# Layer 0 opened feature tile by feature tile: modulation columns of 128 features, and six gate tiles that follow each one

## The chip, the cores and the metric

The kernel runs on one core of a Trainium2 chip. The metric is device time in microseconds, the median of repeated runs. Engines are called as in the profile: PE (TensorE, matmuls; PEld its weight loads), DVE (VectorE), ACT (ScalarE), POOL (GpSimd), and SP, which issues most DMAs. [...]

## The reference

A two-layer backbone over 1024 latent tokens and 256 context tokens of 1024 features: layer 0 is windowed attention, layer 1 a bidirectional state-space mixer. What matters here is how layer 0 begins:

```python
mod = jax.nn.silu(cond) @ w + b          # cond: c (latent) or c_ctx (context); 3 x 1024 columns
shift, scale, gate = jnp.split(mod, 3, axis=-1)
u  = rms_normalize(h)  * (1.0 + scale[:, None]) + shift[:, None]
uc = rms_normalize(hc) * (1.0 + scale_c) + shift_c
q, k, v, g = jnp.split(h @ w_in, ...)    # of u and of uc; g is used as silu(g)
```

`rms_normalize` divides each token by the root of its mean square over the 1024 features.

## The kernel before

Activations lie with features on the 128 partitions, as eight feature tiles k = 0..7, and tokens along the free axis, in three token tiles: 0 and 1 (latent, 512 tokens each) and 2 (the context, 256 tokens). Every operand of a large product is split into a hi part and the rest (`uH`, `uL` for activations, `wh`, `wl` for weights), and a product is three matmuls: hi x hi, hi x lo and lo x hi (`mm3`, L227 to L229). A weight is loaded into a `wr` buffer (seven), cast to hi by ACT (L213) and reduced to its low part by POOL or DVE (L215); `wh` and `wl` have four buffers each, reused in turn. An engine's order is settled ahead of the run by a scheduler that works on a modelled timeline; `issue_after` and `high_priority` bend it.

`norm0` is the opening. It loads tile 0 of x and the modulation weights in blocks of 512 output columns (`load_ada`: four blocks of 2 MiB, shift in blocks 0 and 1, scale in 2 and 3). `ada0` multiplies a block by the two condition vectors: eight matmuls of 512 columns into four strips of 32 PSUM rows, a copy to SBUF (`arow`, L374) and four small sums (`modulation`, L201) that turn it into columns. `stats` squares a token tile on ACT and adds the eight squares, on DVE for tile 0 and on POOL for tiles 1 and 2; `rstd_c` makes sums over partitions on PE (L348), root (ACT, L356), reciprocal and a diagonal (DVE, L359), and a product with ones (PE, L361) that spreads the factor `rr` over all partitions. The eight feature tiles are then modulated in two halves of four, each half once its two blocks of columns are there. Behind each half come half the products of G0 = 4 gate tiles (`g_out` takes tanh and writes them to DRAM). The rest of the gate tiles for tile 0, and all for tile 2, are made at the end of `qkvg`.

Tiles 1 and 2 are normalised while PE makes keys and values of tile 0. `modulate` does one feature tile of one token tile (with `pool=True` POOL takes the multiplication by `rr`). `qkvg` then runs over the token tiles, keys (two products) and then values (one per 128 tokens), and after that the queries and the remaining gates, with the modulation of later stages (`adaln_col`) in between. The tiles `v`, `kHH`, `kL` lie in a pool that opens where the opening's pool `n0` closes, so their first writes wait for the last readers there. PSUM has four banks for products (`pj`).

Of the kernel before, what the change touches and what calls it, by code (L numbers as in the profile page):

```python
# [47 lines left out]
VLAST = 0  # L48
G0 = 4
N0P = (0, 4, 8)  # L50
U0OFF = (0, -200, -100)
AHEAD = 1
# [53 lines left out]
class Kernel:  # L106
# [18 lines left out]
    def build(self):  # L125
# [11 lines left out]
        self.eps = t(cp, [P, 1], F32, "eps")  # L137
        nc.vector.memset(self.eps, EPS)

        self.ptag = "pt"  # L140
        self.mod = [t(cp, [P, 24, 2], F32, f"mod{i}") for i in range(2)]
# [15 lines left out]
    def load_cond(self, p):  # L157
        nc, t, cp = self.nc, self.t, self.cp
        cc = t(p, [P, KT, 2], F32, "cc")
        nc.sync.dma_start(cc, self.a["cc"].rearrange("p (k c) -> p k c", k=KT))  # L160
        th = t(p, [P, KT, 2], F32, "cth")
        nc.scalar.activation(th, cc, AF.Tanh, scale=0.5)
        nc.vector.tensor_scalar_mul(cc, cc, 0.5)
        cs = self.csf = t(cp, [P, KT, 2], F32, "cs")
        nc.vector.scalar_tensor_tensor(cs, in0=th, scalar=1.0, in1=cc, op0=ALU.add, op1=ALU.mult)

        self.sel = t(cp, [P, 2], F32, "sel")
        nc.vector.tensor_reduce(self.sel, self.ident.rearrange("p (j r) -> p r j", r=32)[:, 0:2], axis=mybir.AxisListType.X, op=ALU.add)
        self.bada = t(cp, [P, 2, 24], F32, "bada")
        nc.sync.dma_start(self.bada, self.a["bada"].rearrange("p (l t) -> p l t", l=2))  # L170

    def adaln_col(self, layer, n, pool, ps):
# [23 lines left out]
    def modulation(self, layer, n, row, ps):  # L196

        nc = self.nc
        mt = self.t(ps, [P, 512], F32, "pt")
        for j in range(4):  # L200
            nc.tensor.matmul(mt[:, 2 * j : 2 * j + 2], row[:, j * P : (j + 1) * P], self.sel, start=True, stop=True)  # L201
        m = self.mod[layer][:, n * 4 : n * 4 + 4, :]
        nc.vector.tensor_tensor(m, mt[:, :8].rearrange("p (a b) -> p a b", b=2), self.bada[:, layer, n * 4 : n * 4 + 4].unsqueeze(2).broadcast_to([P, 4, 2]), op=ALU.add)
        if n // 2 == 1:
            nc.vector.tensor_scalar_add(m, m, 1.0)
        return m
# [74 lines left out]
    def modulate(self, layer, h, r, i, k, pool=False):  # L281
# [11 lines left out]
        else:  # L293
            nc.vector.scalar_tensor_tensor(h, in0=h, scalar=sc, in1=r, op0=ALU.mult, op1=ALU.mult)
            nc.scalar.activation(uh, h, AF.Identity, bias=sh)
            nc.vector.scalar_tensor_tensor(ul, in0=h, scalar=sh, in1=uh, op0=ALU.add, op1=ALU.subtract)

# [67 lines left out]

    def ada0(self, n, raw, ps):

        nc, t = self.nc, self.t
        pj = t(ps, [P, 512], F32, "aps", 2)
        for k in range(KT):  # L370
            j = k % 4
            nc.tensor.matmul(pj[32 * j : 32 * j + 32], self.cs[:, k, :], raw[k // 2][:, k % 2], start=k < 4, stop=k >= 4)
        row = t(self.p0, [P, 512], F32, "arow")
        nc.scalar.copy(row, pj)  # L374
        self.modulation(0, n, row, ps)

    def norm0(self, c0, p):


        nc, t, a = self.nc, self.t, self.a  # L380
        ps = self.psA
        p1 = self.p0 = self.pool("n0", ctx=c0, side="right")

        u = self.up
        hin, hs = {}, {}
        raws = {}

        def load_x(i):
            src = self.xin(i).rearrange("(k p) n -> p k n", p=P)
            if i == 0:  # L390
                x = t(u, [P, KT, 512], F32, "uL1")
                hin[i] = [x[:, :4], x[:, 4:]]
            elif i == 1:
                hin[i] = [t(u, [P, KT // 2, 512], F32, tag) for tag in ("uH2", "uL2")]
            else:
                hin[i] = [t(p1, [P, 2, 512], F32, "wada").rearrange("p k n -> p (k n)").rearrange("p (k n) -> p k n", k=4) for _ in range(2)]
            hs[i] = [x[:, k] for x in hin[i] for k in range(4)]
            for e in range(2):
                ld = nc.sync.dma_start(hin[i][e], src[:, 4 * e : 4 * e + 4])
            return ld  # L400

        def load_ada(n):
            raws[n] = [t(p1, [P, 2, 512], F32, "wada") for e in range(4)]
            for e in range(4):
                ld = nc.sync.dma_start(raws[n][e], self.a["w_ada"][0, n, 2 * e : 2 * e + 2].rearrange("k p c -> p k c"))
            return ld

        def stats(i):
            n = TT[i][1]
            acc = t(p1, [P, 512], F32, "sqa")[:, :n]  # L410
            for k in range(KT):
                if k == 0:
                    nc.scalar.activation(acc, hs[i][k], AF.Square)
                else:
                    sq = t(p1, [P, 512], F32, "sqt")[:, :n]
                    nc.scalar.activation(sq, hs[i][k], AF.Square)
                    (nc.vector if i in (0,) else nc.gpsimd).tensor_tensor(acc, acc, sq, op=ALU.add)
            return self.rstd_c(p1, acc, n, D)

        def gates(e):  # L420
            return [self.load_w(a["wg"][x][:, e * 512 : (e + 1) * 512], 4, eng=nc.gpsimd) for x in range(G0)]

        last = lambda: self.tc.issue_after(ld.ins)
        load_x(0)
        load_ada(0)
        ld = load_ada(2)
        with last():
            wg = gates(0)
        r = stats(0)
        for k in range(KT):  # L430
            nc.vector.tensor_mul(hs[0][k], hs[0][k], r)
        self.alloc_u(0)
        m = self.mod[0]
        for e in range(2):
            for n in (e, 2 + e):
                self.ada0(n, raws[n], ps)
            for k in range(4 * e, 4 * e + 4):
                h, uh = hs[0][k], self.uH[0][:, k, :]
                nc.vector.tensor_scalar(out=h, in0=h, scalar1=m[:, 8 + k, 0:1], scalar2=m[:, k, 0:1], op0=ALU.mult, op1=ALU.add)
                nc.scalar.copy(uh, h)  # L440
                nc.vector.tensor_sub(self.uL[0][:, k, :], h, uh)  # L441
            if e == 0:
                pj = [t(ps, [P, 512], F32, "pj") for _ in range(G0)]
            for x in range(G0):
                self.mm3(pj[x], [(wg[x][0][:, k], wg[x][1][:, k], self.uH[0][:, 4 * e + k, :], self.uL[0][:, 4 * e + k, :]) for k in range(4)], e == 0, e == 1)
                if e == 1:
                    self.g_out(p, pj[x], x, 0)
            if e == 0:
                load_ada(1)
                ld = load_ada(3)  # L450
                with last():
                    wg = gates(1)
                    wk = [self.load_halves(a["wk"][x], nc.gpsimd) for x in range(2)]
                    ld = load_x(1)
                with last():
                    self.load_rope(p, 0, LAT)
                    load_x(2)
        for i in (1, 2):
            with self.tc.high_priority(offset=-U0OFF[i]):
                r = stats(i)  # L460
                self.alloc_u(i)
                for k in range(KT):
                    self.modulate(0, hs[i][k], r, i, k, N0P[i] > k)
        return wk
# [11 lines left out]
    def load_rope(self, p, s, n):  # L476
# [3 lines left out]
        self.nc.sync.dma_start(self.cos, self.a["cos"][:, s : s + n])  # L480
        self.nc.sync.dma_start(self.sin, self.a["sin"][:, s : s + n])

# [23 lines left out]
    def g_out(self, p, pj, x, i):  # L506
        nc, t = self.nc, self.t
        n = TT[i][1]
        th = t(p, [P, 512], F32, "qf")[:, :n]
        nc.scalar.activation(th, pj[:, :n], AF.Tanh, scale=0.5)  # L510
        nc.vector.scalar_tensor_tensor(th, in0=th, scalar=1.0, in1=pj[:, :n], op0=ALU.add, op1=ALU.mult)
        nc.sync.dma_start(self.sg_d[x // 2][i][x % 2], th)

    def q_step(self, p, w, x, i):
# [972 lines left out]
def layout(i):  # L1487
# [10 lines left out]
    d["cc"] = np.ascontiguousarray(cc.reshape(KT, P, 2).transpose(1, 0, 2)).reshape(P, -1)  # L1498
    d["w_ada"] = np.ascontiguousarray(i["w_ada"].reshape(2, KT, P, 6, 512).transpose(0, 3, 1, 2, 4))
    d["bada"] = np.ascontiguousarray(i["b_ada"].reshape(2, 24, P).transpose(2, 0, 1)).reshape(P, 48)  # L1500
    w = i["attn_w_in"][0]
# [3 lines left out]
    perm = np.concatenate([np.arange(h * HD, (h + 1) * HD) for j in range(KV) for e in range(2) for h in (4 * j + e, 4 * j + 2 + e)])  # L1505
    d["wg"] = tiles(w[:, 1536:][:, perm])
    d["wo"] = tiles(i["attn_w_out"][0][perm])
    d["sink"] = np.ascontiguousarray(i["attn_sink"].reshape(1, HEADS))
# [43 lines left out]
```

## Time and profile before

| | us |
|---|---|
| median of 3 runs | 1890.34 |
| lowest, highest run | 1886.82, 1890.70 |
| span of the profiled execution | 1886.0 |
| PE busy in it | 1790.8 |

The profiled execution's own time is its span, first to last instruction; nothing else of it is listed. It lies 0.8 us below the fastest run and 4.3 below the median. A profile row names line, engine, operation, the tile written and the tiles read; "idle before" is how long the engine had stood still, with the instruction or DMA that released it. Starts are in microseconds from the span's start.

### The profile page before, as it was taken

What the parts mean: (1) busy time and instruction counts of PE and PEld (TensorE: products, weight loads), DVE (VectorE), ACT (ScalarE), POOL (GpSimd) and SP (SyncE); (2) the same over time, 40 slices, a digit from 0 to 9 for tenths busy, and PEclk for the clock granted to TensorE, in tenths of its full rate; (3) what the DMA queues carried; (4) which work ended last, traced back from release to release, by engine and by line L of the source; (5) the groups of instructions that cost most, each with busy time, mean ns of one, the idle gap of its engine ahead of it and who ended that gap; (6) DMA issues with size and microseconds to landing.
All of it is one profiled execution on the core that took longest, in us unless ns stands there. A gap on an engine that the chain in (4) does not pass through costs nothing. (4 is left out here: it accounts for less than half of the span.)

```text
span 1886.0 us, 29647 instructions
## 1 busy us (share of the span) xinstructions
PE 1790.8 (95%) x10632; PEld 1543.2 (82%) x10632; DVE 1186.5 (63%) x2214; ACT 906.5 (48%) x1863; POOL 751.1 (40%) x1026
## 2 busy tenths in 40 slices
PE   6779998899999899879999999999999999999997
PEld 3678776788889787668898898989889898988887
DVE  4753425887777766584665757666575766754743
ACT  4522225677787765472353534434353543543532
POOL 2731105664456464302334352524335252442411
PEclk9889999999999999989999999999999999999998
DMA  9338765653345456220111111111111111433552
GB/s 358 111 79 251 233 209 132 143 124 95 96 118 135 112 137 198 87 55 23 49 36 44 44 36 44 36 44 36 43 47 33 44 39 41 138 119 100 176 162 68
DMA packets 147204, 192.10 MB, mean 102 GB/s; under 512 B 15313, under 2 KB 84817, under 8 KB 147057
## 3 DMA queue, kind: packets, MB, share of 16 engines
q1 hardware_dynamic: 112992, 171.56, 29.1%
q0 software_dynamic: 34064, 18.65, 5.6%
q8 instruction: 84, 1.38, 0.3%
q14 instruction: 64, 0.52, 0.1%
HBM read 154.54 MB, written 35.92 MB: 101 GB/s over the span
## 5 line engine op out<-in xcount | busy, mean ns | idle before, releaser
L227 PE MATMUL pj<-uH,wh 128*128 128x512 f32 (+1 forms) x712 | 258.8, 365 | 27.1 <-DVE v L549 9.5
L228 PE MATMUL pj<-uL,wh 128*128 128x512 f32 (+1 forms) x712 | 245.6, 345 | 1.5 <-DVE uL L441 1.2
L229 PE MATMUL pj<-uH,wl 128*128 128x512 f32 (+1 forms) x712 | 245.0, 344 | 1.3 <-POOL wl L215 1.3
L1066 POOL TENSOR_TENSOR xw<-xn,dtdec 128x256 f32<-128x256 f32 x144 | 106.4, 741 | 205.7 <-PE psD L1089 102.5
L227 PEld LDWEIGHTS pj<-uH,wh 128*128 128x128 f32 x712 | 136.9, 193 | 55.8 <-issue 19.1
L991 PE MATMUL pj<-uH,wh 128*128 128x512 f32 x512 | 171.7, 405 | 0.8 <-ACT xn L958 0.8
L991 PE MATMUL pj<-uH,wl 128*128 128x512 f32 x512 | 171.7, 404 | 0.0
L991 PE MATMUL pj<-uL,wh 128*128 128x512 f32 x512 | 168.7, 399 | 0.0
L215 POOL TENSOR_TENSOR wl<-wr,wh 128x512 fp32r<-128x512 f32 x96 | 125.7, 1313 | 97.9 <-ACT wh L213 97.2
L1016 PE MATMUL pj<-wh,uH 128*128 128x256 f32 x512 | 154.7, 302 | 0.0
L638 DVE TENSOR_TENSOR pl<-pt,ph 128x512 fp32r<-128x512 f32 x168 | 114.4, 688 | 63.5 <-ACT ph L637 62.8
L1016 PE MATMUL pj<-wh,uL 128*128 128x256 f32 x512 | 151.4, 296 | 0.0
L1016 PE MATMUL pj<-wl,uH 128*128 128x256 f32 x512 | 151.0, 295 | 0.0
L229 PEld LDWEIGHTS pj<-uH,wl 128*128 128x128 f32 x712 | 136.3, 192 | 17.7 <-POOL wl L215 1.7
L228 PEld LDWEIGHTS pj<-uL,wh 128*128 128x128 f32 x712 | 137.1, 193 | 15.7 <-DVE uL L441 3.6
L213 ACT CAST wh<-wr 128x512 fp32r<-128x512 f32 (+1 forms) x136 | 86.9, 644 | 124.7 <-PE pj L228 88.0
L1195 ACT ACTIVATE uT<-psX,nw 128x128 f32<-128x128 f32 x128 | 47.0, 367 | 189.8 <-PE psX L1194 188.6
L612 DVE CUSTOM_DVE_ANT_0 sm<-S,mask,nsink 128x640 f32<-128x640 f32 (+2 forms) x160 | 119.2, 772 | 23.2 <-PE S L609 11.9
L637 ACT CAST ph<-pt 128x512 fp32r<-128x512 f32 x168 | 97.3, 585 | 61.3 <-PE pt L633 55.6
L614 ACT ACTIVATE sm<-sm,nm 128x640 f32<-128x640 f32 (+2 forms) x160 | 118.6, 742 | 11.0 <-DVE nm L612 10.4
L1161 POOL TENSOR_TENSOR xs<-xn,sk 128x256 f32<-128x256 f32 x64 | 42.0, 656 | 184.7 <-DVE sk L1157 183.4
L991 PEld LDWEIGHTS pj<-uL,wh 128*128 128x128 f32 x512 | 95.6, 188 | 19.9
(332 smaller groups left out, 4994.8 us busy)
## 6 DMA issues: line engine op xcount, KB each, us to landing
wr<-w_x SPq DMA_DIRECT2D x32, 512.0 KB
wr<-wo SPq DMA_DIRECT2D x48, 256.0 KB
wr<-w_sk SPq DMA_DIRECT2D x24, 512.0 KB
wr<-wg SPq DMA_DIRECT2D x40, 256.0 KB
qs<-q POOLq DMA_DIRECT2D x40, 256.0 KB, 3.9
wada<-w_ada SPq DMA_DIRECT2D x16, 512.0 KB
wr<-wq SPq DMA_DIRECT2D x32, 256.0 KB
wl<-w_ada SPq DMA_DIRECT2D x32, 256.0 KB
```

Of the source, the lines that this page charges most:

```text
L213: nc.scalar.copy(h, raw)
L215: (eng or nc.vector).tensor_tensor(l, raw, h, op=ALU.subtract)
L227: self.nc.tensor.matmul(ps, lh, rh, start=first and i == 0, stop=False)
L228: self.nc.tensor.matmul(ps, lh, rl, start=False, stop=False)
L229: self.nc.tensor.matmul(ps, ll, rh, start=False, stop=last and i == n - 1)
L612: nc.vector.tensor_tensor_reduce(out=sm[:, :W], in0=Sv, in1=self.mask[:, m0 : m0 + W], scale=-SCALE, scalar=self.nsink[:, 4 * j + r : 4 * ...
L614: nc.scalar.activation(sm[:, :W], sm[:, :W], AF.Exp, bias=nm[:, r : r + 1], scale=-1.0, accum_out=sums[:, r : r + 1])
L637: nc.scalar.copy(ph, ptf)
L638: nc.vector.tensor_sub(pl, ptf, ph)
L991: nc.tensor.matmul(raw[:, 512 * i : 512 * i + 512], l[:, k, :], r[i][:, k, :], start=k + y == 0, stop=k == KT - 1 and y == 2)
L1016: nc.tensor.matmul(pj[:, c], l, r[:, k, :], start=c % 2 + q + k + y == 0, stop=c % 2 == 1 and q == 1 and k == 3 and y == 2)
L1066: nc.gpsimd.tensor_tensor(xw, X(st, c).rearrange("p (r h) -> p r h", r=R), self.dtdec[:, c, hd(d, g)].unsqueeze(2).broadcast_to([P, R, HP] ...
```

## The change

Only the opening is rewritten; everything from the keys of tile 0 on is the same code, with G0 = 6 instead of 4.

- The modulation weights are laid out anew (`w_ad0`): block k holds the 128 shift and the 128 scale columns of feature tile k, 1 MiB. One block makes one feature tile's columns: eight matmuls of 256 columns (`strips`), a copy, two small sums (`sums`), one add on DVE. The 1 of 1 + scale is put into the bias once.
- The gate weights are laid out by feature tile too (`wg0`: four gate tiles, `wg1`: the fifth and sixth, two feature tiles at a time). As soon as feature tile k of token tile 0 is modulated, six gate products take it up (18 matmuls, `gates`), so they add up over k in six PSUM banks. Strips for k + 2 stand between the third and the fourth of them, the sums behind the sixth.
- The modulation of tile 0 by `rr` and scale is one DVE operation (`modulate`) instead of two.
- The sums of squares of tiles 1 and 2 come from copies of x and ctx with tokens on the partitions (`xn`, `ctxn`, together 3 MiB of added loads): one ACT pass per 128 tokens with a running sum, six in all.
- The root and reciprocal are one power on POOL, for all three tiles.
- All loads of the opening stand in one written order on SP (`fetch`).
- PSUM has six `pj` and two `aps` banks.

The core of the diff:

```diff
-G0 = 4
+G0 = 6
...
-        BUFS.update(S=1, pj=4, wr=7, qf=2, ql=2, wh=4, wl=4)
+        BUFS.update(S=1, pj=6, aps=2, wr=7, qf=2, ql=2, wh=4, wl=4)
...
+        def load(k):
+            raws[k] = t(p1, [P, KT, 2 * P], F32, "wada", 3)
+            fetch(raws[k], a["w_ad0"][k].rearrange("p (k c) -> p k c", k=KT))
+            four[k] = weight(a["wg0"][k])
+            if k % 2 == 0:
+                two[k // 2] = weight(a["wg1"][k // 2])
...
+        def strips(k):
+            st[k] = t(ps, [P, 512], F32, "aps")
+            for q in range(KT):
+                j = q % 4
+                nc.tensor.matmul(st[k][32 * j : 32 * j + 32, : 2 * P], self.cs[:, q, :], raws[k][:, q], start=q < 4, stop=q >= 4)
+            row = t(p1, [P, 2 * P], F32, "arow", 2)
+            nc.scalar.copy(row, st[k][:, : 2 * P])
...
+        def spread(i, rc, n):
+            nb = n // P
+            nc.gpsimd.tensor_tensor(rc[:, :nb], rc[:, :nb], self.mhalf[:, :nb], op=ALU.pow)
...
+        def square(i, b, ss):
+            x = tok[i, b]
+            nc.scalar.activation(x, x, AF.Square, scale=1.0 / 32.0, accum_out=ss[:, b : b + 1])
...
+        for k in range(KT):
+            op = self.modulate(0, hs[0][k], rr[0], 0, k)
+            with gates(k, range(0, 3)):
+                if k + 2 < KT:
+                    strips(k + 2)
+            if k + 1 < KT:
+                split(k + 1)
+            if k + 3 < KT:
+                load(k + 3)
+            if 1 <= k < 5:
+                load_tok(1, k - 1)
+            if 3 <= k < 7:
+                with self.tc.issue_after(self.cast.ins):
+                    square(1, k - 3, ss1)
...
+            with gates(k, range(3, G0)):
+                if k + 2 < KT:
+                    sums(k + 2)
...
+        with self.tc.issue_after(op.ins):
+            for k in range(4):
+                self.modulate(0, hs[1][k], rr[1], 1, k)
+        outs = [self.g_out(p, pj[x], x, 0) for x in range(G0)]
...
+        for k in range(4, KT):
+            with self.tc.issue_after(outs[k - 2].ins):
+                self.modulate(0, hs[1][k], rr[1], 1, k)
+        with self.tc.issue_after(outs[-1].ins):
+            for b in range(2):
+                square(2, b, ss2)
+            mean(ss2, CTX)
+            spread(2, ss2, CTX)
+            self.alloc_u(2)
             for k in range(KT):
...
+                self.modulate(0, hs[2][k], rr[2], 2, k)
```

Where instructions stand, for three places. PE at the first gate products before (`aps` and `pt` are modulation PSUM tiles, `wada` the modulation weights, `pj_292` to `pj_295` four gate tiles):

```order
L201 MATMUL pt_256<-sel_108,arow_254 128x2 x4
L372 MATMUL aps_262<-wada_167,cs_35_119 32x512 x2
L372 MATMUL aps_262<-wada_168,cs_35_119 32x512 x2
L372 MATMUL aps_262<-wada_169,cs_35_119 32x512 x2
L201 MATMUL pt_273<-sel_108,arow_271 128x2 x4
L372 MATMUL aps_420<-wada_344,cs_35_119 32x512 x2
L227 MATMUL pj_292<-uH_94_243,wh_176 128x512
```

and the same place now (`pj_254` on are the six gate tiles; lines are those of the changed kernel, L413 `strips`, L421 `sums`, L468 to L470 `gates`, L430 the product that spreads `rr`):

```order
L451 MATMUL aps_202<-ones_68,sqa_179 128x1 x4
L430 MATMUL aps_212<-sqt_210,ones_68 128x512
L413 MATMUL aps_224<-wada_163,cs_36_122 32x256 x8
L413 MATMUL aps_238<-wada_169,cs_36_122 32x256 x8
L421 MATMUL aps_224<-sel_110,arow_233 128x2 x2
L421 MATMUL aps_238<-sel_110,arow_247 128x2 x2
L468 MATMUL pj_254<-uH_91_252,wh_216 128x512
```

Two blocks of 512 columns stood ahead of the first gate product, with a third begun; now two blocks of 256 do, and the norm ahead of them.

ACT in the gate steps of the changed kernel (`wh` casts of gate weights L212, hi casts of the modulated tile L294, copies of modulation rows L415, squares of token rows L436):

```order
L415 COPY arow_326<-aps_317 128x256
L212 CAST wh_379<-wr_291 128x512
L294 ACTIVATE uH_91_252<-uL_61_158,mod_5_74 128x512
L212 CAST wh_424<-wr_338 128x512
L294 ACTIVATE uH_91_252<-uL_61_158,mod_5_74 128x512
L436 ACTIVATE tok_342,ss_260<-tok_342 128x1024
L415 COPY arow_377<-aps_368 128x256
L212 CAST wh_428<-wr_340 128x512
L415 COPY arow_422<-aps_413 128x256
L212 CAST wh_476<-wr_385 128x512
L294 ACTIVATE uH_91_252<-uL_61_158,mod_5_74 128x512
```

`wh_379` takes the buffer that the fifth and sixth gate tile of step 1 read last, and `wh_476` that of step 3; the hi casts for steps 2 and 4 stand behind them.

DVE ahead of the values of tile 0 before (`wada_417` here is the context, `v` the values' tile, whose subtraction L549 frees a `pj` bank):

```order
L290 TENSOR_SCALAR wada_417<-wada_417,mod_4_72 128x256
L292 TENSOR_TENSOR uL_183_634<-wada_417,uH_182_633 128x256 x2
L535 COPY kL_189_676<-ql_740 128x512
L535 COPY kL_190_677<-ql_781 128x512
L549 TENSOR_TENSOR v_671<-pj_796,v_671 128x4x64
```

and now:

```order
L293 SCALAR_TENSOR_TENSOR x_176_670<-x_176_670,mod_5_74,rr_181_696 128x256 x8
L555 TENSOR_TENSOR ql_838<-qf_837,qh_839 128x512
L295 SCALAR_TENSOR_TENSOR uL_183_699<-x_176_670,mod_5_74,uH_182_698 128x256 x8
L534 TENSOR_TENSOR qf_986<-pj_961,cos_548 128x512
L535 STREAM_SHUFFLE rope_b_989<-pj_961 128x512
L599 COPY kL_189_733<-ql_797 128x512
L599 COPY kL_190_734<-ql_838 128x512
L613 TENSOR_TENSOR v_728<-pj_853,v_728 128x4x64
```

In both, the values wait behind the whole context; now two reads of the keys of tile 1 (`pj_961`) stand ahead of them as well, which have a bank of their own.

More of the change, by code (lines that the diff above doesn't have):

```diff
@@ L48 @@
 VLAST = 0
-G0 = 4
-N0P = (0, 4, 8)
-U0OFF = (0, -200, -100)
+G0 = 6
 AHEAD = 1
@@ L198, in modulation @@
         nc = self.nc
-        mt = self.t(ps, [P, 512], F32, "pt")
+        mt = self.t(ps, [P, 512], F32, "aps")
         for j in range(4):
@@ L364, in rstd_n @@
         return r
[L366 to L375, printed above, removed]
     def norm0(self, c0, p):
         nc, t, a = self.nc, self.t, self.a
[L381 to L410, printed above, removed]
-            for k in range(KT):
[L412 to L463, printed above, removed]
@@ new lines, in norm0 @@
+        pn = t(ps, [P, 512], F32, "aps")
+        for b in range(4):
+            nc.tensor.matmul(pn[:, b : b + 1], acc[:, b * P : (b + 1) * P], self.ones[:, 0:1], start=True, stop=True)
+        rc = t(p1, [P, 4], F32, "ss", 3)
+        nc.vector.tensor_scalar(out=rc, in0=pn[:, :4], scalar1=1.0 / D, scalar2=EPS, op0=ALU.mult, op1=ALU.add)
+        spread(0, rc, 512)
+        split(0)
+        strips(0)
+        sums(0)
+        strips(1)
+        sums(1)
+        self.alloc_u(0)
+        pj = [t(ps, [P, 512], F32, "pj") for _ in range(G0)]
```

101 lines of the change are left out of this document (94 added, 7 removed).

## The prediction

> **What bounds the kernel now.** I read the page's first part, then the busy times by stage, then TensorE's own timeline around each hole.
>
> ```profile
> PE 1790.8 (95%) x10632; PEld 1543.2 (82%) x10632; DVE 1186.5 (63%) x2214; ACT 906.5 (48%) x1863; POOL 751.1 (40%) x1026
> ```
>
> TensorE is idle for 1886.0 - 1790.8 = 95.2 us in all. The stages (columns: PE, PEld, DVE, ACT, POOL busy with counts, granted PE clock, DMA share, GB/s) tell where:
>
> ```profile
> 0.00:28.60 28.60, 14.27 (x62) 5.50 (x62) 15.03 (x29) 11.87 (x20) 4.51 (x9) 1.00 0.94 340
> 28.60:42.40 13.80, 13.80 (x52) 9.39 (x52) 4.99 (x7) 3.62 (x6) 5.56 (x5) 0.88 1.05 387
> 42.40:60.00 17.60, 12.36 (x58) 8.03 (x58) 10.22 (x11) 9.80 (x18) 12.94 (x11) 0.71 0.57 206
> 60.00:86.50 26.50, 26.22 (x140) 22.16 (x138) 16.52 (x20) 15.25 (x26) 18.68 (x15) 1.00 0.37 121
> 86.50:93.00 6.50, 0.73 (x4) 0.73 (x4) 6.50 (x9) 2.79 (x5) 5.07 (x6) 0.83 0.00 0
> 93.00:101.50 8.50, 8.43 (x51) 8.20 (x50) 4.81 (x8) 2.54 (x4) 2.56 (x3) 0.73 0.17 63
> 101.50:111.20 9.70, 0.20 (x2) 0.00 (x0) 9.56 (x20) 4.33 (x12) 9.14 (x14) 0.65 0.37 63
> 123.90:286.80 162.90, 162.90 (x1057) 132.92 (x1056) 60.15 (x121) 40.43 (x77) 25.07 (x29) 1.00 0.70 214
> 286.80:300.00 13.20, 6.20 (x30) 4.13 (x30) 5.08 (x20) 5.29 (x16) 4.69 (x8) 0.83 0.68 161
> ```
>
> From 123.9 to 286.8 TensorE has no hole at all, so whatever the opening gives up arrives at 286.8 undiminished unless data are late. The opening holds 14.3 us of idleness up to 28.6, 5.2 up to 60, 5.8 up to 93 and 9.5 up to 111.2, and stretches at half clock. In the timeline (start, duration, idle before and its releaser):
>
> ```profile
> 28.60 1.45 PE L227 MATMUL pj<-uH,wh 128*128 128x512 f32 x4 [2.33 <-ACT uH L440]
> 33.52 0.39 PE L227 MATMUL pj<-uH,wh 128*128 128x512 f32 x1
> 33.75 0.39 PE L228 MATMUL pj<-uL,wh 128*128 128x512 f32 x1
> 51.35 2.07 PE L227 MATMUL pj<-uH,wh 128*128 128x512 f32 x4 [3.00 <-ACT uH L440]
> 54.59 0.79 PE L228 MATMUL pj<-uL,wh 128*128 128x512 f32 x1 [1.17 <-DVE uL L441]
> 55.61 0.63 PE L227 MATMUL pj<-uH,wh 128*128 128x512 f32 x1
> 56.03 0.63 PE L228 MATMUL pj<-uL,wh 128*128 128x512 f32 x1
> 92.27 1.01 PE L348 MATMUL pt<-ones,sqa 128*128 128x1 f32 x4 [5.78 <-POOL sqa L417]
> 111.24 0.77 PE L227 MATMUL pj<-uH,wh 128*128 128x512 f32 x1 [9.54 <-DVE v L549]
> 123.83 0.28 PE L227 MATMUL pj<-wh,uH 128*128 128x256 f32 x1
> 123.94 0.28 PE L228 MATMUL pj<-wl,uH 128*128 128x256 f32 x1
> ```
>
> Matmuls of 512 columns start 0.227 us apart at full clock (33.52 to 33.75), 0.42 at half (55.61 to 56.03); of 256 columns 0.12. I take 123.83, the first matmul on tile 1's values, as the mark: the same work follows it in both kernels, except that gate tiles 4 and 5 for tile 0 no longer do.
>
> **The change, step by step: first gate matmul.** Prices:
>
> ```profile
> 9.86 2.19 ACT L416 ACTIVATE sqt<-uL 128x512 f32<-128x512 f32 x4 [0.59 <-DMA uL<-xT]
> 8.27 5.47 DVE L417 TENSOR_TENSOR sqa<-sqa,sqt 128x512 f32<-128x512 f32 x7 [4.59 <-ACT sqt L416]
> 14.38 1.87 PE L348 MATMUL pt<-ones,sqa 128*128 128x1 f32 x8
> 16.80 0.69 DVE L359 TENSOR_TENSOR sqt<-ident,rc 128x512 f32<-128x512 f32 x1
> 18.05 1.65 PE L361 MATMUL pt<-sqt,ones 128*128 128x512 f32 x2
> 21.59 1.91 PE L372 MATMUL aps<-wada,cs 128*32 128x512 f32 x12
> 42.45 2.78 PE L372 MATMUL aps<-wada,cs 128*32 128x512 f32 x24
> 45.16 1.05 PE L201 MATMUL pt<-sel,arow 128*128 128x2 f32 x8
> 24.79 5.66 POOL L215 TENSOR_TENSOR wl<-wr,wh 128x512 fp32r<-128x512 f32 x4 [23.40 <-ACT wh L213]
> L1178 POOL TENSOR_TENSOR ss<-ss,half 128x1 f32<-128x1 f32 x64 | 37.8, 590 | 147.2 <-ACT y L1177 147.2
> 74.60 0.72 ACT L295 ACTIVATE uH<-uL,mod 128x512 fp32r<-128x512 f32 x1
> ```
>
> x tile 0 is still in by 9.86, now in four pieces, so only the last two squares (0.55 each) and one sum (0.78) come after it: about 12.0 instead of 13.7. Column sums on PE (1.87): 13.9. The root is now a power on POOL, and it stands there behind the first weight split. That weight lies 1.25 MiB behind x: at 387 GB/s it lands at 13.3, cast at 13.9, split (1.41) at 15.3. The power of 128x4 has no row; 128x1 takes 0.59, so it is between 0.59 and four times that, 2.4; I take 1.5, the middle, since a part of 0.59 is fixed: 16.8. Diagonal 0.69, product 1.65: 19.2. Two strips follow, each 16 records of 256 columns; at 0.16 for 512 columns (1.91 over 12) that is 1.3 a strip: 21.8. Sums, add, modulate (0.69), cast (0.72) and hand-overs: first gate matmul at 25.0, against 28.60. Gone from ACT are six table loads, and from DVE eight multiplications by rr; neither stood on this path except the root's.
>
> **Gates.** 144 matmuls x 0.227 = 32.7. Six strips lie between them: 16 records each, at half of 0.116 (2.78 over 24) = 0.93, so 5.6; if a record costs the same at 256 columns, 11.1. Six pairs of sums, four records of 0.13 (1.05 over 8): 3.1. Half clock in the first 4 us costs 2.0. The order has a weight cast ahead of the hi cast in steps 2, 4 and 6, and that cast's buffer comes free only at the end of the step before: cast 0.62 and 0.72, less the sums that cover 0.5, about 1.0 us three times, 3.0. The product for tile 1's norm 0.5. Together 46.9: gates end at 71.9. DMA is no end here: the last modulation piece lies at 14.25 MiB, and (14.25 - 2) x 1.0486 / 0.387 = 33.2 us after 9.86 is 43, while its strip stands in step 5, after 50. The 3 MiB of added token rows (8 us of transfer) so cost nothing on this path; if the queue stood still for 8 us or more, they would.
>
> **To the mark.** Keys of tile 0 48 x 0.227 = 10.9, values 96 x 0.12 = 11.5, the product for the context norm 0.3, keys of tile 1 10.9: 33.6. The mark is at 105.5 if nothing waits.
>
> **What is late next.** After the gates VectorE has tile 1, the gate outputs, two ropes, the context, then the values that free PSUM for the mark:
>
> ```profile
> 72.91 6.21 DVE L294 SCALAR_TENSOR_TENSOR uL<-uL,mod,rr 128x512 f32<-128x512 f32 x4 [0.31 <-ACT rr L363]
> 79.65 4.03 DVE L296 SCALAR_TENSOR_TENSOR uL<-uL,mod,uH 128x512 fp32r<-128x512 f32 x3
> 84.06 0.74 DVE L296 SCALAR_TENSOR_TENSOR uL<-uL,mod,uH 128x512 fp32r<-128x512 f32 x1
> 108.79 0.40 DVE L290 TENSOR_SCALAR wada<-wada,mod 128x256 f32<-128x256 f32 x1
> 110.01 0.75 DVE L535 CAST kL<-ql 128x512 fp32r<-128x512 f32 x2
> 110.68 1.08 DVE L549 TENSOR_TENSOR v<-pj,v 128x256 fp32r<-128x256 f32 x3
> ```
>
> Undisturbed: 16 operations on tile 1 at 0.74 = 11.8; four gate outputs, four rope reads, two adds and two subtractions, all 512 wide, at 0.7 = 8.4; diagonal 0.4; 16 on the context at 0.40 = 6.4; two more rope reads 1.4; two casts 0.75; the first value 0.4: 29.6. Started 2 us after the gates' end, behind three casts on ACT, it ends at 103.5, two before the mark. So TensorE decides, narrowly. The hole of 9.54 us closes because six PSUM banks instead of four let the keys of tile 1 pass ahead of the values. The sums of squares of tile 1 and context leave POOL (hole of 5.78); they are now one ACT pass per 128 tokens, six in all, between casts that have cover in a gate step of 5.5 us; without that cover each would delay a hi cast by its own length.
>
> **Sum.** The mark moves by 105.5 - 123.8 = -18.3. Behind it two gate tiles are gone, 48 x 0.227 = -10.9. Given back: six gate tiles in a row that are left with the context only, instead of four, each with 1.4 MiB of transfers (3.8 us at 387 GB/s) beside some 3.6 us of PE; between 0 and 4 us, I take 1, since stage 123.90 stands at a DMA share of 0.70. Together -28, so 1858 for the profiled execution. Its span of 1886.0 is 4.3 below the median of 1890.34; against that median the forecast is 1862.
>
> [...] Between 42.4 and 60 the holes of 3.00 and 1.17 us were followed by matmuls 0.42 apart up to 60: some 4 us of loss. [...]
>
> **Rivals.** (A) VectorE decides at the mark. For: the same operation took 1.55 (6.21 over 4) and 1.34 (4.03 over 3) while POOL multiplied, 0.74 alone; POOL has eight splits (8 x 1.41 = 11.3 us) beside this chain. If they double what runs beside them, up to 11 us more: chain 114.5, and 1.5 for half clock after the hole: -18.6 and 1872. Against: up to half of those splits come before the chain starts. [...] (B) Slower: the clock stays at half through the gates, since each step leans on ACT and DVE. 144 x (0.42 - 0.227) = 27.8, strips and sums double, +8.7: 36.5 - 28 = +8.5, 1899. It decides from three quarters of the gates on. For: stage 42.40 with its 0.71. Against: there TensorE was idle 30%; a step here has 5.5 us of PE against some 3 each of DVE and ACT. (C) The gain is given back at the start of attention, where 286.80 to 300.00 already has 7.0 us idle: no change, 1890. For: loads there end that wait. Against: they are issued when PE frees the buffers, so they come as much earlier.
>
> **How the numbers follow.** Forecast (mark between 99 and 112, -20 to -35) 0.72; A 0.15; B 0.06; C 0.03; 0.04 for a gain between C's and A's. Bounds: power 0.9 either way, strips +5.5, cast waits 3 less or 3 more, contention +11, DMA +3. Low 1852 (-38: no cast waits, cheap start, no DMA loss, and a median nearer the fast run), high 1875 takes in A. The forecast's own range is 1854 to 1870. A measurement tells about 0.2%, 3.8 us, from no change. Faster 0.91, same 0.03, slower 0.06.
>
> **What would show it.** Right: first gate matmul near 25; clock 1.0 from 30 on; gate steps of 5.5 us, ending near 72; the mark at 103 to 108; no hole over 2 us before it; the same 150 us of full PE behind it. Wrong: gate steps over 8 us, a granted clock near 0.5 between 30 and 70, a hole before the mark released by DVE v, or holes among the context-only gate tiles released by DMA.

## The result, and the profile after

The changed kernel takes 1860.50 us (median of 4 runs, 1859.69 to 1863.18), the kernel before 1890.52 beside it: ratio 0.9837, 95% interval [0.9822, 0.9851], 30 us faster. The forecast was 1862. The profiled execution took 1859.69 and has a span of 1858.0, 28.0 below that of before; the prediction's sum was -28. Busy times first, then the stages (columns as in the prediction):

```profile
PE 1778.6 (96%) x10684; PEld 1537.0 (83%) x10684; DVE 1176.4 (63%) x2208; ACT 902.9 (49%) x1858; POOL 731.7 (39%) x1007
```

```profile
0.00:26.08 26.08, 8.78 (x50) 4.92 (x51) 9.68 (x23) 10.79 (x18) 6.83 (x11) 1.00 0.79 295
26.08:72.00 45.92, 45.92 (x265) 32.88 (x265) 15.08 (x24) 19.73 (x37) 15.35 (x12) 0.96 0.87 318
72.00:107.80 35.80, 35.15 (x201) 30.70 (x200) 33.58 (x56) 17.67 (x36) 15.13 (x13) 1.00 0.40 136
107.80:258.60 150.80, 149.38 (x1007) 123.65 (x1006) 61.81 (x125) 39.19 (x76) 29.14 (x36) 1.00 0.80 239
258.60:272.00 13.40, 11.32 (x45) 9.20 (x45) 6.04 (x23) 8.08 (x27) 7.61 (x12) 0.75 0.79 186
```

From the first gate matmul to 72.0 PE has no idle time at all, and 0.65 us of it in the next 36; before, there were some 20 us of it between 28.6 and 111.2. VectorE is now busy 94% of the stage up to the mark (33.58 of 35.80). PE's timeline, in the rows that the forecast named:

```profile
12.46 1.87 PE L451 MATMUL aps<-ones,sqa 128*128 128x1 f32 x8 [12.46 <-DVE sqa L448]
17.75 2.07 PE L430 MATMUL aps<-sqt,ones 128*128 128x512 f32 x2 [3.42 <-DVE sqt L428]
26.08 1.91 PE L468 MATMUL pj<-uH,wh 128*128 128x512 f32 x6 [1.42 <-ACT uH L294]
...
39.85 1.63 PE L468 MATMUL pj<-uH,wh 128*128 128x512 f32 x6
42.78 1.07 PE L413 MATMUL aps<-wada,cs 128*32 128x256 f32 x16
71.32 1.02 PE L430 MATMUL aps<-sqt,ones 128*128 128x512 f32 x2
72.41 0.40 PE L470 MATMUL pj<-uH,wl 128*128 128x512 f32 x1
84.36 0.39 PE L226 MATMUL pj<-wh,uH 128*128 128x256 f32 x1 [0.65 <-DVE qf L574]
107.34 0.28 PE L226 MATMUL pj<-wh,uH 128*128 128x256 f32 x1
118.85 0.28 PE L226 MATMUL pj<-uH,wh 128*128 128x256 f32 x1
```

First gate matmul at 26.08, last at 72.41, mark at 107.34 (123.83 before), and the context's keys at 118.85 (135.34 before). Of the 28.0 us, 16.5 are won ahead of the mark; 10.9 are the two gate tiles that no longer follow it (48 matmuls at 0.227, not measured apart), and the 0.6 that remain are less than two runs of one kernel differ by.

### The profile page after: what moved, and what is told of

It reads as the page before. It is cut to its first block, busy times and chain, and to the rows that moved or that the text cites. A ratio compares the mean times of both kernels' runs of the same rounds, so it can differ in the third digit from the quotient of the medians.

```text
span 1858.0 us, 29740 instructions
## 1 busy us (share of the span) xinstructions
PE 1778.6 (96%) x10684; PEld 1537.0 (83%) x10684; DVE 1176.4 (63%) x2208; ACT 902.9 (49%) x1858; POOL 731.7 (39%) x1007
## 5 line engine op out<-in xcount | busy, mean ns | idle before, releaser
L226 PE MATMUL pj<-uH,wh 128*128 128x256 f32 (+1 forms) x664 | 236.9, 357 | 5.7 <-DVE xn L1510 1.9
L228 PE MATMUL pj<-uH,wl 128*128 128x256 f32 (+1 forms) x664 | 224.5, 338 | 2.0 <-POOL wl L214 2.0
L227 PE MATMUL pj<-uL,wh 128*128 128x256 f32 (+1 forms) x664 | 224.1, 337 | 0.4 <-POOL uL L720 0.4
L214 POOL TENSOR_TENSOR wl<-wr,wh 128x512 fp32r<-128x512 f32 x100 | 132.1, 1324 | 109.7 <-ACT wh L212 103.6
L226 PEld LDWEIGHTS pj<-uH,wh 128*128 128x128 f32 x664 | 126.3, 190 | 28.8 <-issue 7.8
L212 ACT CAST wh<-wr 128x512 fp32r<-128x512 f32 (+1 forms) x140 | 89.8, 643 | 106.2 <-PE pj L227 78.1
L228 PEld LDWEIGHTS pj<-uH,wl 128*128 128x128 f32 x664 | 125.9, 190 | 17.7 <-POOL wl L214 3.2
L227 PEld LDWEIGHTS pj<-uL,wh 128*128 128x128 f32 x664 | 126.6, 191 | 11.3 <-issue 1.1
L1055 PEld LDWEIGHTS pj<-uL,wh 128*128 128x128 f32 x512 | 95.6, 188 | 19.9
```

The costliest lines, as they stand in the source:

```text
L212: nc.scalar.copy(h, raw)
L214: (eng or nc.vector).tensor_tensor(l, raw, h, op=ALU.subtract)
L226: self.nc.tensor.matmul(ps, lh, rh, start=first and i == 0, stop=False)
L227: self.nc.tensor.matmul(ps, lh, rl, start=False, stop=False)
L228: self.nc.tensor.matmul(ps, ll, rh, start=False, stop=last and i == n - 1)
L1055: nc.tensor.matmul(raw[:, 512 * i : 512 * i + 512], l[:, k, :], r[i][:, k, :], start=k + y == 0, stop=k == KT - 1 and y == 2)
```

## The experiments

Each was timed beside the kernel before on the same chip, so ratios are compared. "Start" is the first matmul on the context's keys, less 10.9 us where two more gate tiles stand ahead of it than in the kernel before (these are then missing behind it). "Rest" is the span less that start.

| kernel | median, us | ratio, 95% interval | start | rest |
|---|---|---|---|---|
| before | 1890.5 to 1893.1 | 1 | 135.3 | 1750.7 |
| changed | 1860.50 | 0.9837 [0.9822, 0.9851] | 108.0 | 1750.0 |
| before, token-row norms | 1885.28 | 0.9956 [0.9942, 0.9971] | 126.5 | 1751.7 |
| before, six banks | 1878.73 | 0.9930 [0.9917, 0.9943] | 124.5 | 1753.6 |
| before, six banks, six gate tiles | 1869.44 | 0.9877 [0.9861, 0.9894] | 120.2 | 1748.5 |
| changed, four gate tiles, four banks | 1876.68 | 0.9911 [0.9896, 0.9926] | 121.1 | 1751.4 |
| changed, four gate tiles | 1865.22 | 0.9850 [0.9836, 0.9865] | 111.0 | 1753.1 |
| changed, feature-major norms | 1865.38 | 0.9862 [0.9844, 0.9880] | 112.5 | 1753.1 |
| changed, once more | 1859.33 | 0.9831 [0.9807, 0.9856] | 108.3 | 1749.7 |
| changed, 24 matmuls more | 1865.31 | 0.9860 [0.9838, 0.9881] | 113.6 | 1746.6 |
| changed, 8 DVE products more | 1863.88 | 0.9863 [0.9841, 0.9885] | 113.7 | 1748.4 |
| warm-up, 30 matmuls | 1852.49 | 0.9796 [0.9773, 0.9819] | 104.7 | 1747.4 |
| warm-up, 38 matmuls | 1853.54 | 0.9794 [0.9777, 0.9811] | 104.9 | 1747.6 |
| warm-up, diagonal on ACT | 1855.27 | 0.9806 [0.9792, 0.9821] | 103.1 | 1747.9 |

The starts lie 32 us apart and the rests within 7: what the opening gives up arrives at the end, in every version, to within those 7 us.

**Four gate tiles in the opening.** One edit of the changed kernel, the two tiles left where they were:

```diff
-G0 = 6
+G0 = 4
```

> The changed kernel with four gate tiles in its opening instead of six (tiles 4 and 5 are made later again; PSUM banks stay six). Theory, TensorE decides the opening: the gates end 10.9 us earlier (48 matmuls x 0.227) and the same 10.9 us come later, so the time is that of the changed kernel within 3 us, 1858 to 1864, and the mark (first value matmul of tile 1) lies near 96.4 instead of 107.3. Rival, the chain from modulation strips to hi casts or the loads set the pace of a step, and the two tiles ride along unpaid: the mark stays near 107 and the time is some 11 us longer, 1871.

0.9850 against 0.9837: some 2.5 us, within the intervals. The rival (11 us longer) is out, but the mark is at 99.44 instead of 96.4. Gate steps of four tiles are too short to cover the chain to the hi cast: PE waits 1.99, 0.72 and 0.39 us in them, and the longest wait is followed by half clock from some 38.2 to 41.7 (products 0.43 apart from 38.74 to 40.45, 0.23 from 43.57), which costs some 1.7; the first gate matmul, 1.7 earlier, gives that much back.

```profile
36.90 1.19 PE L464 MATMUL pj<-uH,wh 128*128 128x512 f32 x4 [1.99 <-ACT uH L294]
```

So where the two tiles stand is neutral but for some 3 us: with six tiles a step these waits are covered.

**The same with four banks.**

```diff
-        BUFS.update(S=1, pj=6, aps=2, ...
+        BUFS.update(S=1, pj=4, aps=2, ...
```

> As the kernel with four gate tiles, with four PSUM banks for products instead of six. Theory, the hole of 9.54 us closed because of the two added banks: the keys of tile 1 wait again for VectorE to release the values of tile 0, a hole of 6 to 10 us ahead of the mark and a stretch at half clock behind it, so 7 to 11 us longer than with six banks. Rival, the hole closed because the context's norm no longer stands on POOL: the same time as with six banks, within 2 us.

11.5 us above the version with six (0.9911 - 0.9850 = 0.0061), a little over the range. A part of the hole of before is back, released by the same instruction, and the keys of tile 1 start behind it:

```profile
96.26 0.79 PE L226 MATMUL pj<-uH,wh 128*128 128x512 f32 x1 [5.36 <-DVE v L609]
```

**Before, with norms of tile 1 and context from token rows.** ACT's running sums over `xn` and `ctxn`, loaded behind x of the same tile, replace the eight squares and POOL's sums.

> The kernel before, with one part of the change: the sums of squares of tiles 1 and 2 come from token rows by one ACT pass per 128 tokens (3 MiB of added loads); root, halves, four gate tiles and four banks stay (one buffer of squares fewer). Theory: the hole of 5.78 us (released by the sum on POOL) goes with the half clock behind it, and the context's chain on VectorE, which holds the hole of 9.54 us, begins earlier: 6 to 14 us shorter, 1876 to 1884. Rival, all of the gain comes from the feature tiles and the wait only moves to the next thing on VectorE: within 3 us of the kernel before.

8.3 us. POOL's hole of 5.78 is gone and the mark comes 8.9 earlier, but the hole released by the values is still there, now 10.60:

```profile
101.35 0.79 PE L227 MATMUL pj<-uH,wh 128*128 128x512 f32 x1 [10.60 <-DVE v L562]
```

**Before, with six banks and six gate tiles.**

```diff
-G0 = 4
+G0 = 6
-        BUFS.update(S=1, pj=4, wr=7, ...
+        BUFS.update(S=1, pj=6, aps=2, wr=7, ...
```

To make room, the norms' and the modulation's small tiles (`pt` and `aps`) share two banks, here and in the next version.

> The kernel before with six gate tiles in its two halves instead of four, six PSUM banks for products and two shared ones. Theory: modulation by halves leaves the holes ahead of each half as they are (14 us up to the first gate matmul, 5 ahead of the second half), but the two tiles fill TensorE while tile 1 and the context are normalised, so the holes of 5.78 and 9.54 us shrink: 5 to 11 us shorter, 1880 to 1885. Rival, the added casts and splits of gate weights delay the norms by as much: within 3 us of the kernel before.

A miss: 23 us instead of 5 to 11, three quarters of the whole gain with the old order by halves and the old norms. The next version splits it.

**Before, with six banks alone.**

> The kernel before with six PSUM banks for products instead of four (the two of the norms and the two of the modulation sums become two shared ones), and nothing else: still halves, feature-major norms, four gate tiles. The kernel before with six banks and six gate tiles took 23.7 us off, far more than the 5 to 11 that I had expected; this run splits that. Theory (the banks close the hole of 9.5 us and its half clock, the tiles the rest by covering VectorE and the loads): 10 to 14 us below the kernel before, no hole over 2 us ahead of tile 1's values. Rival (the banks alone do it): 20 to 24 below. Rival (the tiles alone): within 3 us of the kernel before.

13.2 us, inside the theory's range; the other 10 came with the tiles. The 13 are net of a loss: with the shared banks the norm of tile 0 stands ahead of the strips, and the first gate matmul comes at 34.41 instead of 28.60. PE's longest waits in its first 300 us (waited for, us in total, times, longest), behind the wait for x:

```profile
PE aps L348 <- POOL sqa L417: 4.5, 1, 4.5
PE pj L227 <- ACT uH L440: 3.6, 1, 3.6
PE aps L201 <- DVE mod L203: 3.3, 1, 3.3
PE pj L227 <- ACT wh L213: 3.3, 1, 3.3
```

The wait for the values (9.54) is gone, as the theory said; that no hole over 2 us would stay ahead of the mark was wrong, since POOL's sum still holds PE 4.5. The two extra gate tiles then give PE work over such waits: with them POOL's hole shrinks to 2.48,

```profile
100.27 0.61 PE L348 MATMUL aps<-ones,sqa 128*128 128x1 f32 x4 [2.48 <-POOL sqa L417]
```

and the wait on the weight cast at the start of attention (3.3, L213) is not in that kernel's list of waits. By the table 4.3 us of the ten lie ahead of the start and 5.1 behind it.

**Feature-major norms in the changed kernel.** ACT squares the feature tiles of x and ctx, POOL adds seven times per tile, PE sums over features; the token rows aren't loaded.

> The changed kernel with the norms of tile 1 and the context from feature-major rows again: ACT squares eight pieces, POOL adds them up, TensorE sums over features; the token rows are not loaded, and x of tile 1 is fetched in their place. Theory (the token rows matter through POOL: seven sums for the context stand behind the key splits there): tile 1's norm is hidden behind the gates, the context's is ready 3 to 6 us later than now, the mark moves from 107.4 to 110 to 114, time 3 to 7 us above the changed kernel's. Rival (hidden anyway, since the gates cover it): mark within 1 us of 107.4, time the same within 1 us.

0.9862 against the 0.9837 and 0.9831 of the changed kernel's two comparisons: 5 to 6 us, with intervals that overlap at their edges; the start is 4.6 later. The context's norm is late, as the theory said, and by more: its product stands at 103.67 instead of 94.53. The mark is hardly later (108.01, not 110 to 114). The wait comes at the second value product, for a rope read that stands behind most of the context on VectorE:

```profile
103.67 0.59 PE L430 MATMUL aps<-sqt,ones 128*128 128x256 f32 x2
113.18 0.38 PE L226 MATMUL pj<-wh,uH 128*128 128x256 f32 x1 [2.14 <-DVE rope_b L544]
```

Set against the old order with six banks, six tiles and such norms (0.9877), this version has the rest of the rewrite: the order by feature tiles and, with it, the layouts, the power on POOL, the single modulation operation and the order of the loads. All of that is 0.0015, inside both intervals.

**Who decides at the mark.** The changed kernel once more, as a yardstick; then with more work on PE, and with more on VectorE:

> The changed kernel once more, as the yardstick for the three kernels that run beside it. Every theory: ratio to the kernel before 0.983 to 0.985, the first matmul on tile 1's values at 107.3 us, first gate matmul at 26.1.

```diff
-        for q in range(parts):
+        for q in [0] * (rep - 1) + list(range(parts)):    # rep = 2 for the first keys of tile 0
```

> The changed kernel with the product for tile 0's first keys made twice: 24 more matmuls of 512 columns on TensorE ahead of the mark, 24 x 0.227 = 5.4 us; VectorE's work is unchanged. Theory (TensorE's own work sets the mark): the mark moves from 107.3 to 112.8, no hole there, and the time is 5 to 6 us above the changed kernel's. Rival (VectorE's chain, which ends at 107.6, sets it, and TensorE has slack that the trace does not show): mark at 107.5 to 109, time 0 to 2 us above.

```diff
+        for _ in range(8):
+            with self.tc.issue_after(op.ins):
+                op = nc.vector.tensor_tensor(acc, rr[0], rr[1], op=ALU.mult)
```

> The changed kernel with eight more 512-wide products on VectorE between tile 1 and the context, 8 x 0.68 = 5.5 us; TensorE's work is unchanged. The prediction gave VectorE's chain 2 us of slack at the mark; the trace of the changed kernel shows it level with TensorE within 0.3 us. If level: a hole of about 5 us before the mark released by the value subtraction, mark at 112 to 113, half clock behind it for 1.5 us, time 6 to 7 us above the changed kernel's. If 2 us of slack: hole 3.5, time 4 to 5 above. If six banks give far more slack (the rival that VectorE is not near the bound at all): no hole, time unchanged within 1 us.

More matmuls: the start moves by 5.3 (124.50 against 119.16 in the repeat), the time by 6.0 (the profiled spans differ by 2.1 only, and the intervals overlap). More VectorE work: the start moves by 5.4 (124.61), the time by 4.6. The trace gives the reason, and corrects the prediction as well as the expectation:

```profile
102.87 0.68 DVE L537 TENSOR_TENSOR qf<-pj,cos 128x512 f32<-128x512 f32 x1
106.31 0.68 DVE L537 TENSOR_TENSOR qf<-pj,cos 128x512 f32<-128x512 f32 x1
116.32 0.42 DVE L616 TENSOR_TENSOR v<-pj,v 128x256 fp32r<-128x256 f32 x1
```

```profile
106.02 0.28 PE L226 MATMUL pj<-wh,uH 128*128 128x256 f32 x1
116.88 0.55 PE L226 MATMUL pj<-wh,uH 128*128 128x256 f32 x1 [4.53 <-DVE v L616]
```

The mark here is at 106.02, ten microseconds ahead of the first value subtraction. Two value products ran before that subtraction, so their banks were not those of tile 0's values; by elimination they are the two that the ropes of tile 1's keys had read (102.87 and 106.31). The version with feature-major norms names such a bank: its second value product waits for `rope_b` (the row at 113.18). Only the third value product waits for the subtraction here. The subtraction came 9.1 us later than in the changed kernel (107.26) with 5.5 of work added, since the scheduler had also put both rope reads ahead of the context, and some operations took longer (two of the 0.68 us products 1.78, at 91.90 and 95.44; the eight multiplications of the context 4.28 instead of 3.25); 4.5 of that became a hole, and behind it products were 0.21 apart up to 121.08 and 0.12 from 121.27. The expectation named the releaser rightly, and the place wrongly.

**A shorter way to the first gate matmul.** In the changed kernel PE waits 3.42 for the diagonal with strips at hand, the power stands behind a weight split, and products run at twice their later time (2.07 at 17.75, 1.02 at 71.32). Three edits:

```diff
+        for _ in range(30):
+            nc.tensor.matmul(idle[:, :P], self.ones, self.ones, start=True, stop=True)
...
-        spread(0, rc, 512)
-        split(0)
-        strips(0)
-        sums(0)
+        strips(0)
+        sums(0)
+        with self.tc.issue_after(spread(0, rc, 512).ins):
+            split(0)
```

> The changed kernel with three edits in the first 26 us: 30 matmuls of 128x128 without use while TensorE waits for x; the strips and sums of features 0 to 127 ahead of the product that spreads the norm; the power on POOL ahead of the first weight split. Theory (the changed kernel's first gate matmul is late through half clock and through the order of that chain, and what is won there arrives at the end): column sums at 12.4 take 0.95 instead of 1.87, power by 14.6, diagonal 0.7, product 1.0, copy 0.6, modulate 0.75, cast 0.8: first gate matmul at 18.5 to 20 instead of 26.1, at full clock, mark near 99 to 101, time 6 to 9 us below the changed kernel's. Rival (the transfers set the pace: the gates run beside a DMA share of 0.87, and 22.3 MB by their end need 58 us at 387 GB/s): gates wait for strips and weights, end no earlier than 69, time 0 to 3 us below. Rival (the extra matmuls outlast the wait for x): column sums later than 12.5, and each us later costs one.

6.8 us below the repeat, with intervals that overlap by 0.0012; the first gate matmul is at 21.93 instead of 26.26, the mark at 104.06 instead of the theory's 99 to 101. It did not go the theory's way:

```profile
1.13 9.15 PE L446 MATMUL pj<-ones 128*128 128x128 f32 x60 [1.13 <-DVE mhalf L138]
12.54 1.87 PE L455 MATMUL aps<-ones,sqa 128*128 128x1 f32 x8 [2.26 <-DVE sqa L452]
14.34 1.93 PE L413 MATMUL aps<-wada,cs 128*32 128x256 f32 x16
...
17.66 2.05 PE L430 MATMUL aps<-sqt,ones 128*128 128x512 f32 x2
```

After 9 us of matmuls and a hole of 2.26 the column sums take 1.87 again. The windows of this version show the clock (third number from the end of each row):

```profile
5.00:10.30 5.30, 5.28 (x44) 5.09 (x43) 2.87 (x5) 3.77 (x7) 0.00 (x0) 1.00 1.06 414
10.30:12.50 2.20, 0.00 (x0) 0.00 (x0) 1.98 (x3) 1.09 (x2) 0.00 (x0) 1.00 0.99 394
12.50:16.30 3.80, 3.73 (x24) 2.38 (x24) 0.69 (x2) 1.23 (x2) 1.61 (x2) 0.51 1.06 425
16.30:19.70 3.40, 2.94 (x10) 1.43 (x14) 1.38 (x2) 0.37 (x1) 2.34 (x2) 0.50 0.99 396
19.70:21.90 2.20, 1.88 (x17) 0.54 (x16) 0.75 (x1) 1.85 (x4) 0.97 (x1) 0.50 1.11 428
21.90:24.00 2.10, 2.07 (x9) 1.76 (x9) 0.89 (x1) 0.75 (x2) 1.62 (x2) 0.78 0.99 339
```

The gain is therefore that of the order, as far as the trace shows: strips under the diagonal's wait, the power ahead of the split. A version with the order and no warm-up matmuls is missing. The first rival's waits for transfers are not there: the two waits in the gates, 0.60 and 0.27, are released by ACT and DVE, though the gates end at 69, as it said. Of it 3.6 us stand at the context's keys (115.57 against 119.16); the profiled spans differ by 5.9, and the spreads of the runs (1849.7 to 1855.4 and 1855.7 to 1863.5) leave room for either.

**Warm-up until the squares are summed (38 matmuls).**

> The version with warm-up matmuls, now 38 of them instead of 30, so that they last until the squares are summed at 12.4 us: in the run with 30 they ended at 10.3, a hole of 2.26 us followed, and everything from 12.5 to 22.5 ran at half clock. Theory (that hole cost the clock): column sums take 0.95 instead of 1.87, the two strips 1.0 each instead of 1.9, first gate matmul at 19 to 20.5 instead of 21.9 and at full clock, mark at 100.5 to 102 instead of 104.1, time 2 to 4 us below that version's. Rival (the clock falls anyway, by the short waits between 13 and 20): everything as with 30, time the same within 1 us, or later by what the extra matmuls overrun.

```profile
12.44 1.05 PE L455 MATMUL aps<-ones,sqa 128*128 128x1 f32 x8 [0.30 <-DVE sqa L452]
13.42 1.07 PE L413 MATMUL aps<-wada,cs 128*32 128x256 f32 x16
14.98 0.61 PE L421 MATMUL aps<-sel,arow 128*128 128x2 f32 x4 [0.49 <-ACT arow L415]
16.74 2.05 PE L430 MATMUL aps<-sqt,ones 128*128 128x512 f32 x2 [1.15 <-DVE mod L422]
18.72 1.94 PE L413 MATMUL aps<-wada,cs 128*32 128x256 f32 x16
```

The first half of the theory held (sums 1.05, strips 1.07), the second didn't: after waits of 0.49 and 1.15 the product takes 2.05 again. The first gate matmul comes at 21.01, 0.9 earlier, and the time is the same (0.9794 and 0.9796).

**The diagonal of tile 0 on ACT, with 38 warm-up matmuls.**

> As the version with 38 warm-up matmuls, and the diagonal of tile 0's norm made on ACT in four pieces of 128x128 instead of on VectorE, where it took 1.75 us beside a weight split on POOL and 0.69 alone. Theory (the diagonal stands on the path to the first gate matmul): 0.5 to 1 us earlier at the mark than with the diagonal on VectorE, time 0 to 1.5 us lower. Rival (the weight casts now stand behind it on ACT, and the first low part comes late): first gate step stretched, 0 to 1.5 us higher.

The mark comes 1.2 us earlier than with the diagonal on VectorE (102.44 against 103.62); the time is not lower (0.9806 against 0.9794, each inside the other's interval). Whether it gives anything stays open. The version with 38 matmuls is faster than the kernel before; its interval ends at 0.9811, the changed kernel's begins at 0.9822 in the first comparison and at 0.9807 in the second, so some 7 us below the changed kernel are likely and not certain.

## Why the prediction was right, point by point

- **The sum.** -28 forecast, -28.0 in the profiled execution, with the parts: mark -18.3 forecast, -16.5 measured; two gate tiles -10.9 in both, by the same arithmetic; +1 given back forecast, -0.6 left over. Small errors of both signs met, so that the sum is right to a tenth is luck.
- **First gate matmul**, 25.0 forecast, 26.08 measured. The power took less than the 1.5 assumed (1.03 for 128x4, where 128x1 took 0.59), the diagonal beside a weight split on POOL more than its 0.69:

```profile
14.88 1.03 POOL L426 TENSOR_TENSOR ss<-ss,mhalf 128x4 f32<-128x4 f32 x1
```

```profile
15.95 1.75 DVE L428 TENSOR_TENSOR sqt<-ident,ss 128x512 f32<-128x512 f32 x1 [1.41 <-POOL ss L426]
66.60 0.68 DVE L428 TENSOR_TENSOR sqt<-ident,ss 128x512 f32<-128x512 f32 x1
```

  and the two strips took 3.64 instead of 2.6, at half speed. The steps as such were right; the warm-up versions show what their order cost.
- **Gates**, 46.9 forecast, 46.3 measured (26.08 to 72.41). From start to start the six strips took 6.9 (5.6 forecast; the bound of 11.1 was not near) and the gate products 36.5 (32.7 and 2.0 for half clock forecast; the clock was half from 27.4 to 30.8, the row 0.96 of that stage). The term of 3.0 for three weight casts was wrong: step 2 (39.85) has no idle time ahead of it, nor has any later step, since PE had enough work left in the step before; with four tiles a step it hadn't, and such waits are there. So the total fits because a wait that was not paid met products that took longer.
- **To the mark**, 33.6 forecast, 34.9 measured (72.41 to 107.34): 0.65 is a hole, the rest lies in small delays between products.
- **"The hole of 9.54 closes because six PSUM banks let the keys of tile 1 pass."** Shown: six banks alone remove that wait, four bring 5.36 back.
- **"What is late next."** "TensorE decides, narrowly" was right: 5.4 us more on PE moved the start by 5.3. The mechanism behind it was partly wrong and did no harm. VectorE's chain, up to the first value, ended at 107.7 instead of 103.5, mainly for contention as in rival A:

```profile
74.09 5.93 DVE L293 SCALAR_TENSOR_TENSOR uH<-uH,mod,rr 128x512 f32<-128x512 f32 x4 [1.35 <-ACT rr L432]
84.23 0.74 DVE L293 SCALAR_TENSOR_TENSOR uL<-uL,mod,rr 128x512 f32<-128x512 f32 x1
...
105.36 0.68 DVE L534 TENSOR_TENSOR qf<-pj,cos 128x512 f32<-128x512 f32 x1
105.97 0.73 DVE L535 STREAM_SHUFFLE rope_b<-pj 128x512 f32<-128x512 f32 x1
107.26 1.07 DVE L613 TENSOR_TENSOR v<-pj,v 128x256 fp32r<-128x256 f32 x3
108.66 0.68 DVE L534 TENSOR_TENSOR qf<-pj,cos 128x512 f32<-128x512 f32 x1
```

  Of the four operations in the first row, three took 1.86, 1.78 and 1.78 beside weight splits on POOL (five, 7.21 us from 71.60); the fourth, behind the splits, took 0.74. With the prediction's reading (the first value frees the bank of the mark) that would have left a hole. But the first subtraction ends at 107.67, after the mark, so the mark's product has another bank: that of the key of tile 1 whose last read, the shuffle, ends at 106.70, 0.64 ahead of 107.34. The second value product, 2.9 later at 110.2, has a bank of tile 0's values: PE's wait on VectorE for it is over at 108.08, before the second key is read at 108.66. VectorE thus had 0.6 us to spare at the mark and 2.5 at the product behind it. Which bank comes next follows the order of VectorE's reads, and that differs between versions: with eight more products both rope reads stand ahead of the values.
- **Holes and the clock.** The sum counts three holes of 1.0 us in the gates at their own length, with no half clock behind them; the changed kernel has no hole in its gates, so its trace doesn't test that. Its opening has one hole at full clock, 1.42 us ahead of the first gate product, and half clock followed from 27.4 to 30.8. Half clock also followed the holes of 1.99 with four gate tiles and of 2.26 with 30 warm-up matmuls; behind the 0.72 with four gate tiles, products were 0.23 apart.
- **Rivals.** A: the contention came, the 11 us did not; its own terms (mark at 114.5, 1.5 of half clock, the two tiles, 1 given back) add up to -17.7, not the -18.6 stated. B: granted clock 0.96 through the gates, no lapse after 30.8. C: nothing is given back at the start of attention, where 258.60 to 272.00 has 2.1 us idle instead of 7.0; at a DMA share of 0.80 PE is busy 149.4 of 150.8 us between the mark and there, context-only gate tiles included.
- **What the prediction didn't see** is how the gain divides. It summed the mark as one path, which gives no share to the single parts. By the runs, going from before to after: six banks 13 us, six gate tiles 10, the order by feature tiles with what comes along 3 (not distinguishable from nothing), token rows 5 (barely distinguishable). In another sequence the shares differ (token rows 8 when first; the new order some 8 between the kernel before with token rows, 0.9956, and the changed one with four tiles and four banks, 0.9911), since each part hides some of the same waits.

## What to carry to other kernels

When an engine waits for another's result at one point, look which buffer it is and who reads it last: here two PSUM banks more gave 13 us that looked like a matter of the order of a whole stage. Move independent large products to where the bound engine has holes: here they were worth 10 us in the old order, and in the new one they cover waits of some 3 us. And test a many-part change by its parts before ascribing its gain: the part that names it can be the smallest.

## What the runs showed of the hardware

- Half clock followed a hole of 1.42 us in the changed kernel (0.50 granted from 27.4 to 30.8), and a hole's length alone doesn't tell whether it does. In the traces of the kernel before and of the changed kernel the clock's records are multiples of 3.41 us long, but for the last of each. Cut into such stretches, full clock gave way to half after none of 1003 with under 0.7 us of PE idleness, after all 12 with over 2.0, and after 8 of the 33 between. A hole of 2.48 (the old order with six banks and six tiles) was followed by full clock, with products of 256 columns 0.12 apart from 100.94.
- In the same two traces it comes back 18 times, each time after a stretch with at most 0.48 us of idleness; two half-clock stretches with 0.37 were followed by another. One stretch of gate products sufficed in the changed kernel (27.4 to 30.8); with 30 warm-up matmuls the clock was half from 12.6 to 22.8, though from 12.54 to 16.27 PE had no idleness, filled with sums over partitions and strips. Whether such narrow products are the reason isn't shown. With 38 the clock was half from 16.1 to 23.0 (0.50 from 16.7 to 20.7).
- The column of the granted clock reads 1.00 where the trace has no record of the clock yet. In the changed kernel the first record begins at 23.9 us; ahead of it the column reads 1.00, while the product in this window takes 2.07, twice the later 1.02. With 30 warm-up matmuls the column reads 1.00 from 0 to 10.3, while 18 matmuls take 3.87 us up to 5.0 (0.215 each) and 44 take 5.28 from there on (0.12 each). Where no record stands, the durations are used here.

```profile
16.00:20.00 4.00, 2.25 (x6) 0.70 (x10) 1.70 (x1) 0.76 (x2) 2.50 (x2) 1.00 0.99 389
```

- In the changed kernel three modulations of 512 columns on VectorE took 1.86, 1.78 and 1.78 us beside weight splits on POOL, and 0.74 behind them; the diagonal of tile 0 took 1.75 beside a split, and 0.69 in the kernel before with nothing on POOL beside it (16.80). Not every operation beside a split took longer: the diagonal at 66.60 took 0.68, the last 0.48 of it beside the split from 66.80 on.
